# One input of the modulation products moved to PSUM in the first feed-forward, and the second parts of its up weights to GpSimd

## The chip, the cores and the metric

The kernel runs on one core of a Trainium2 chip. The metric is the device time of one execution in microseconds. A core has TensorE (PE, matmuls into PSUM; PEld is its loading of weights), VectorE (DVE), ScalarE (ACT), GpSimd (POOL), and SyncE (SP), which issues the DMAs here. SBUF is the working memory; PSUM is the memory that TensorE writes, used here as eight banks of 128 x 512 floats.

## The reference

Two layers over 512 latent tokens of width 1024; 256 context tokens go into the first layer's mixer only. Each layer scales and shifts its input by columns worked out from a vector c (the modulation), runs a mixer (gated DeltaNet and pooling in the first layer, convolutions in the second), normalizes, runs a feed-forward and normalizes again. What the change touches are the modulation and the first feed-forward:

```python
mod = silu_c @ ada_w[layer] + ada_b[layer]            # silu_c: 1024, ada_w: 1024 x 6144 for each layer
sh_m, sc_m, gt_m, sh_f, sc_f, gt_f = [m[:, None, :] for m in jnp.split(mod, 6, axis=-1)]
...
a, gate = jnp.split(u @ w_up, 2, axis=-1)             # w_up: 1024 x 5632
y = (jax.nn.silu(_dwconv2d_grid(a, conv_w)) * gate) @ w_down
```

The convolution is depthwise, 3 x 3, over the 512 tokens as a grid of 8 x 64.

## The kernel before

All arrays stand with channels on the 128 partitions and the 512 tokens along the row. A product of full precision is made of three matmuls in a reduced format: each weight and each activation is split into a first part (the value rounded to the format, names ending in hi or h) and a second part (what the rounding left, names ending in lo or l), and each 128 x 128 block of weights is multiplied as hi x h, hi x l, lo x h (`gemm`, line 219). A weight of the up projection is 128 x 1024 and comes in two pieces of 128 x 512. For each piece SyncE loads `w_raw` (line 159), ScalarE casts it to `w_hi` (line 167), and VectorE or GpSimd subtracts to get `w_lo` (line 173). Which of the two does it is dealt out by a counter: `self.share` is added for each piece, and when the counter reaches 1, VectorE gets the piece. Raw pieces, first parts and second parts have four buffers each.

Up projection of a feed-forward (`ffn`): 22 blocks m, each of two products, `pa` and `pg` (the first three products are made in two halves of 256 tokens, `half_ps`, so that they can start while the normalization before them still works on the second half). Of `pa`, ScalarE makes the middle tap into `f_acc` (line 578), VectorE adds the other eight taps (line 589), ScalarE takes the silu (line 591), VectorE multiplies by `pg` into `f_hid` (line 593), and ScalarE and GpSimd split that into `hh` (line 448) and `hl` (line 449; in the first eight blocks the tiles are called `ah` and `al`).

Modulation: the columns that the first mixer's input needs are made on TensorE at the start. The other 80 columns of 128 (`ada_rest`) are made on VectorE beside other work: a column's weights, 128 x 1024, come as two tiles `ada_w` (line 353), and for each a product with `crow` (the silu of c, the same row on each partition, in SBUF) is taken and summed along the row into one number per partition (line 354). That is one scalar_tensor_tensor with its sum written out, 160 in all; I call it a product here. 24 columns are made in the first mixer and its output projection. In the first feed-forward, blocks m = 2 to 21 make two columns each, so four products behind each `f_hid`, and the first six tiles of the down projection make the other 16. Their order on VectorE is pinned to the order of the program; the rest of the order on each engine is set by a scheduler when the program is built.

PSUM: the eight banks are two rings of four, "0" and "1". `bank` takes them in turn by a pattern of rings: products by "001" in a feed-forward, so two in ring 0 and one in ring 1, and the normalization's small results (`ln_e`, `ln_w`) from ring 1. A bank is free again when its last reader is done.

Down projection (`out_proj`): eight tiles, each over 22 weights; behind them the normalization, whose result goes into the second mixer's input. The shares are 0.1 in the first mixer, 0.35 and 0.5 in the two mixers' output projections, 0.4 in both feed-forwards with 0.5 at their end, 0.1 in the second mixer.

Of the kernel before, what the change touches and what calls it, by code (L numbers as in the profile page):

```python
# [15 lines left out]
T = 512  # L16
# [16 lines left out]
MUL, ADD, SUB = ALU.mult, ALU.add, ALU.subtract  # L33
# [13 lines left out]
SHARE = 0.4  # L47
SHARE_OUT = (0.35, 0.5)
SHARE_ODD = 0.1
SHARE_DOWN = 0.5  # L50
LAST = (4, 4)
LAST_FFN = 2
# [10 lines left out]
EVEN_RINGS = ("0", "1")  # L63
RINGS = ("001", "1")
RINGS_ODD = ("01", "1")
AX0 = 12
AX1 = 8
R2 = 1
# [47 lines left out]
class Kernel:  # L116
# [11 lines left out]
    def constants(self):  # L128
        nc, a = self.nc, self.a
        cp = self.cp = self.pool("const")  # L130
        self.cvec = cp.tile([P, KD, 2], F32, name="cvec")
        nc.sync.dma_start(out=self.cvec, in_=a["cvec"])
        prm = cp.tile([P, a["prm"].shape[1]], F32, name="prm")
        nc.sync.dma_start(out=prm, in_=a["prm"])
        for name, (o, shape) in PARAMS.items():
            n = math.prod(shape)
            v = prm[:, o:o + n]
            if len(shape) == 2:
                v = v.rearrange("p (a b) -> p a b", b=shape[1])
            if len(shape) == 3:  # L140
                v = v.rearrange("p (a b c) -> p a b c", b=shape[1], c=shape[2])
            setattr(self, name, v)
        self.ones = cp.tile([P, P], F32, name="ones")
        nc.vector.memset(self.ones, 1.0)
        self.onesn = cp.tile([P, 2], F32, name="onesn")
        nc.vector.memset(self.onesn, 1.0 / D)
        self.eps = cp.tile([P, 2], F32, name="eps")
        nc.vector.memset(self.eps[:, 0:1], LN_EPS)
        nc.vector.memset(self.eps[:, 1:2], RMS_EPS)

        self.mod = cp.tile([P, 2, 80], F32, name="mod")
        self.ada_next = 0
        self.crow = cp.tile([P, D], F32, name="crow")


# [187 lines left out]
    def ada_rest(self, n, pin=False):  # L343

        nc = self.nc
        if self.ada_next == 0:
            nc.sync.dma_start(out=self.crow, in_=self.a["crow"].broadcast_to([P, D]))
            nc.scalar.activation(out=self.crow, in_=self.crow, func=AF.Silu)
        for i in range(self.ada_next, self.ada_next + n):
            for k in range(2):  # L350
                w = self.ada_tile(k)
                cs = slice(T * k, T * k + T)
                nc.sync.dma_start(out=w, in_=self.a["ada1"][i][:, cs])
                r = nc.vector.scalar_tensor_tensor(out=w, in0=w, scalar=1.0, in1=self.crow[:, cs], op0=MUL, op1=MUL,  # L354
                                                   accum_out=self.mod[:, k, i:i + 1])
                if pin:
                    self.tc.keep_in_program_order(r)
        self.ada_next += n
# [139 lines left out]
    def out_proj(self, src, nk, xh, xl, gt, cols, uh, ul, ahead=0, between=None, ring=None, first=()):  # L498
# [35 lines left out]
        if nk != KD:  # L534
            self.share = SHARE_DOWN
        tick = lambda: norm and next(norm[0], 0)
# [23 lines left out]
    def ffn(self, layer, gt, cols):  # L560
        nc = self.nc
        with ExitStack() as ctx:
            fp = self.pool(f"ffn{layer}", ctx=ctx)
            ring = lambda nm: fp.tile([P, T], F32R, tag="h", bufs=2 * (KF - KD), name=nm)
            temp = lambda i, nm: fp.tile([P, T], F32, tag=("acc", "hid")[i], bufs=2, name=nm)
            self.ada_tile = lambda k: fp.tile([P, T], F32, tag="ada", bufs=ADA_FFN, name="ada_w")
            hh, hl = list(self.ah), list(self.al)
            up = self.a["ffn_up"]
            take = self.products([up[layer, KF * i + m] for m in range(KF) for i in range(2)], ring,
                                 FIRST[2 * layer])  # L570
            for m in range(KF):
                pa, pg = take(), take()
                if m >= KD:
                    hh.append(ring("hh"))
                    hl.append(ring("hl"))
                w = self.fconv[:, layer, m]
                acc = temp(0, "f_acc")
                nc.scalar.activation(out=acc, in_=pa, func=AF.Copy, scale=w[:, 4:5])  # L578
                av = acc.rearrange("p (r c) -> p r c", c=GW)
                sv = pa.rearrange("p (r c) -> p r c", c=GW)  # L580
                for dr in (-1, 0, 1):
                    for dc in (-1, 0, 1):
                        if dr == 0 and dc == 0:
                            continue
                        tap = 3 * (dr + 1) + dc + 1
                        r0, r1 = max(0, -dr), GR - max(0, dr)
                        q0, q1 = max(0, -dc), GW - max(0, dc)
                        o = av[:, r0:r1, q0:q1]
                        nc.vector.scalar_tensor_tensor(out=o, in0=sv[:, r0 + dr:r1 + dr, q0 + dc:q1 + dc],  # L589
                                                       scalar=w[:, tap:tap + 1], in1=o, op0=MUL, op1=ADD)  # L590
                nc.scalar.activation(out=acc, in_=acc, func=AF.Silu)  # L591
                hid = temp(1, "f_hid")
                nc.vector.tensor_tensor(out=hid, in0=acc, in1=pg, op=MUL)
                self.split(hid, hh[m], hl[m])
                next(self.late, 0)
                if layer == 0 and m >= ADA0:
                    self.ada_rest(int(ADA_RATE * (m + 1)) - int(ADA_RATE * m), True)
                if layer == 0 and m == KF - 1:
                    self.columns(1)

            def between(m):
                if layer == 0 and self.ada_next < 80:
                    self.ada_rest(min(ADN, 80 - self.ada_next), True)
                    if self.ada_next == 80:
                        self.columns(2)

            u = (None, None) if cols is None else (self.uh, self.ul)
            self.out_proj(self.a["ffn_down"][layer], KF, hh, hl, gt(), cols, *u, between=between)


    def even(self):
        nc, a = self.nc, self.a
        with ExitStack() as ctx:
# [11 lines left out]
            ps, pooled, self.decays = {}, [], {}  # L625
            left = [[AX0, AX1]]

# [545 lines left out]
    def odd(self):  # L1173
        nc, a = self.nc, self.a
        self.share = SHARE_ODD
        self.rings = RINGS_ODD
        with ExitStack() as ctx:
# [249 lines left out]
```

## Time and profile before

| what | value |
|---|---|
| three timed runs | 1387.52, 1382.17, 1387.93 us (median 1387.52) |
| profiled execution | 1384.9 us |
| its span | 1383.0 us, mean granted TensorE clock 0.967 |
| TensorE busy | 1286.8 us (93%) |
| VectorE busy | 990.9 us (72%) |
| GpSimd busy | 665.0 us (48%) |
| ScalarE busy | 579.8 us (42%) |
| chain that ended last | PE 62%, DVE 22% |
| in the chain by line | PE prod_ps 28%, PE out_ps 20%, DVE ada_w 6%, DVE f_acc 3% |

The span goes from the first to the last instruction of the profiled execution. The chain is followed back from the last instruction, at each step to what released it; the share of an engine in it is the time in which that engine, and nothing else, set the end. A row of a time line has its start and duration in us, the engine, the line of the kernel, the operation, output and input tiles with their shapes, and in brackets how long the engine was idle ahead of it and what ended that. The stages, in us of the span: first mixer to about 343, its output projection to 400, first feed-forward up to 682 and down to 808, second mixer to 961, its output projection to 1001, second feed-forward up to 1244 and down to the end.

### The profile page before, as it was taken

The page shows a single profiled execution, that of the slowest core. Times are in us where ns is not written, and L with a number is a line of the kernel's source. Part 1 is how long each engine was busy: PE and PEld are TensorE (multiplying, and loading weights), DVE is VectorE, ACT ScalarE, POOL GpSimd, SP SyncE. Part 2 cuts the span into 40 slices and gives each one's busy share as a digit, 9 for nine tenths or more (in the row PEclk, how much of TensorE's full clock was granted, in tenths as well). Part 3 has the DMA queues.
Part 4 walks back from the last instruction along what each step waited for, and adds up shares of the span by engine and source line. Part 5 has one row for each costly group of instructions (what it writes and reads, how often), then busy time and mean ns, then how long its engine had stood idle before and what let it go on. Part 6 is the DMA issues. An engine that isn't in the chain of part 4 may idle for free.

```text
span 1383.0 us, 19515 instructions
## 1 busy us (share of the span) xinstructions
PE 1286.8 (93%) x6690; PEld 1075.9 (78%) x6690; DVE 990.9 (72%) x1901; ACT 579.8 (42%) x1089; POOL 665.0 (48%) x580
## 2 busy tenths in 40 slices
PE   6898889989799998988899999899999999999997
PEld 2677878877698776777788888677988888888886
DVE  3388899998688999999955668775676666661125
ACT  3354423446456323323222367545473433332235
POOL 1345456665634444434345665973444344344453
PEclk9899999999899999999999999999999999999998
DMA  9521212430523455544466542232223333233334
GB/s 302 200 69 45 63 43 90 147 115 31 195 95 108 163 172 164 162 159 159 154 193 205 155 135 77 69 100 87 66 77 99 98 94 98 99 90 97 99 111 130
DMA packets 104947, 166.56 MB, mean 120 GB/s; under 512 B 20945, under 2 KB 29201, under 8 KB 104849
## 3 DMA queue, kind: packets, MB, share of 16 engines
q1 hardware_dynamic: 93888, 164.09, 37.5%
q10 hardware_dynamic: 10960, 1.25, 0.6%
q8 instruction: 52, 0.85, 0.2%
q14 instruction: 47, 0.38, 0.1%
HBM read 162.60 MB, written 2.69 MB: 120 GB/s over the span
## 4 chain that ended last, share of the span: by engine, by line
PE 62%; DVE 22%; issue 3%; POOL 3%; ACT 3%; DMA 2%; SPq 0%; ACTq 0%; POOLq 0%; DVEq 0%
PE prod_ps L219 28%; PE out_ps L219 20%; DVE ada_w L354 6%; DVE f_acc L589 3%; PE half_ps L219 3%; DVE w_lo L173 2%; PE ln_e L409 1%; PE qkv_ps L219 1%; PE it_ps L973 1%; PE gate_ps L219 1%; POOL w_lo L173 1%; PE dd_ps L848 1%; DVE z L470 1%; DVE x_t L919 1%; PE iv_ps L981 1%
## 5 line engine op out<-in xcount | busy, mean ns | idle before, releaser
L173 POOL TENSOR_TENSOR w_lo<-w_raw,w_hi 128x512 fp32r<-128x512 f32 (+1 forms) x263 | 358.2, 1368 | 407.9 <-ACT w_hi L167 386.8
L167 ACT CAST w_hi<-w_raw 128x512 fp32r<-128x512 f32 (+1 forms) x408 | 245.1, 607 | 431.0 <-PE prod_ps L219 147.9
L219 PE MATMUL prod_ps<-uh,w_lo 128*128 128x512 f32 x792 | 314.2, 397 | 26.8 <-DVE w_lo L173 20.5
L219 PE MATMUL prod_ps<-uh,w_hi 128*128 128x512 f32 x792 | 312.2, 394 | 0.0
L219 PE MATMUL prod_ps<-ul,w_hi 128*128 128x512 f32 x792 | 311.8, 394 | 0.0
L589 DVE SCALAR_TENSOR_TENSOR f_acc<-prod_ps,prm,f_acc 128x441 f32<-128x441 f32 (+2 forms) x320 | 222.0, 694 | 42.7 <-ACT f_acc L578 34.3
L173 DVE TENSOR_TENSOR w_lo<-w_raw,w_hi 128x512 fp32r<-128x512 f32 (+1 forms) x145 | 118.7, 819 | 126.6 <-ACT w_hi L167 123.3
L219 PEld LDWEIGHTS prod_ps<-uh,w_lo 128*128 128x128 f32 x792 | 151.2, 191 | 64.0 <-DVE w_lo L173 23.7
L354 DVE SCALAR_TENSOR_TENSOR ada_w<-ada_w,crow 128x512 f32<-128x512 f32 x160 | 174.6, 1139 | 4.0 <-DMA ada_w<-in_ada 3.8
L219 PEld LDWEIGHTS prod_ps<-uh,w_hi 128*128 128x128 f32 x792 | 151.3, 191 | 31.7 <-ACT w_hi L167 0.7
L219 PEld LDWEIGHTS prod_ps<-ul,w_hi 128*128 128x128 f32 x792 | 150.9, 191 | 32.0
L219 PE MATMUL out_ps<-ah,w_lo 128*128 128x256 f32 (+1 forms) x352 | 120.3, 342 | 10.0 <-DVE w_lo L173 10.0
L219 PE MATMUL out_ps<-ah,w_hi 128*128 128x256 f32 (+1 forms) x352 | 121.2, 345 | 4.7 <-ACT w_hi L167 3.1
L219 PE MATMUL out_ps<-al,w_hi 128*128 128x256 f32 (+1 forms) x352 | 121.3, 344 | 0.0
L219 PE MATMUL out_ps<-hh,w_lo 128*128 128x512 f32 (+1 forms) x280 | 99.4, 355 | 2.4 <-POOL w_lo L173 1.9
L219 PE MATMUL out_ps<-hh,w_hi 128*128 128x512 f32 (+1 forms) x280 | 98.7, 353 | 0.1
L219 PE MATMUL out_ps<-hl,w_hi 128*128 128x512 f32 (+1 forms) x280 | 98.5, 352 | 0.0
L219 PEld LDWEIGHTS out_ps<-ah,w_lo 128*128 128x128 f32 x352 | 69.0, 196 | 17.6 <-DVE w_lo L173 10.7
L219 PEld LDWEIGHTS out_ps<-ah,w_hi 128*128 128x128 f32 x352 | 68.9, 196 | 12.8 <-ACT w_hi L167 3.5
L449 POOL TENSOR_TENSOR hl<-f_hid,hh 128x512 fp32r<-128x512 f32 x28 | 40.9, 1461 | 75.3 <-ACT hh L448 75.3
L219 PEld LDWEIGHTS out_ps<-al,w_hi 128*128 128x128 f32 x352 | 69.3, 197 | 7.8 <-DVE al L449 0.6
L591 ACT ACTIVATE f_acc<-f_acc 128x512 f32<-128x512 f32 x44 | 27.8, 632 | 107.8 <-DVE f_acc L589 107.8
(359 smaller groups left out, 2316.6 us busy)
## 6 DMA issues: line engine op xcount, KB each, us to landing
ada_w<-in_ada SPq DMA_DIRECT2D x192, 256.0 KB, 3.0
w_raw<-in_ffn_up SPq DMA_DIRECT2D x176, 256.0 KB, 2.7
w_raw<-in_ffn_down SPq DMA_DIRECT2D x100, 256.0 KB, 2.7
w_raw<-in_even_in SPq DMA_DIRECT2D x40, 256.0 KB, 2.8
w_raw<-in_odd_in SPq DMA_DIRECT2D x40, 256.0 KB, 2.7
w_raw<-in_even_out SPq DMA_DIRECT2D x16, 256.0 KB, 2.9
w_raw<-in_odd_out SPq DMA_DIRECT2D x16, 256.0 KB, 2.7
w_raw<-in_ffn_down SPq DMA_DIRECT2D x20, 128.0 KB, 2.2
```

The lines of the kernel that those rows point to most:

```text
L167: r = nc.scalar.copy(out=hi[:, :n], in_=raw)
L173: r = eng.tensor_tensor(out=lo[:, :n], in0=raw, in1=hi[:, :n].bitcast(F32), op=SUB)
L219: r = nc.tensor.matmul(out=o, lhsT=w, rhs=x[k][:, c0:c1], start=clear and k == i == 0, stop=k == n - 1 and i == 2, skip_group_check=pin)
L354: r = nc.vector.scalar_tensor_tensor(out=w, in0=w, scalar=1.0, in1=self.crow[:, cs], op0=MUL, op1=MUL, accum_out=self.mod[:, k, i:i + 1])
L409: nc.tensor.matmul(out=pe[:, 2 * (n * e + i):2 * (n * e + i) + 2], lhsT=t[:, i * P:(i + 1) * P], rhs=ones, start=e == 0 and i == 0 and not ...
L449: (eng or nc.gpsimd).tensor_tensor(out=l, in0=x, in1=h.bitcast(F32), op=SUB)
L470: nc.vector.tensor_tensor(out=z, in0=z, in1=x, op=op)
L589: nc.vector.scalar_tensor_tensor(out=o, in0=sv[:, r0 + dr:r1 + dr, q0 + dc:q1 + dc], scalar=w[:, tap:tap + 1], in1=o, op0=MUL, op1=ADD)
L591: nc.scalar.activation(out=acc, in_=acc, func=AF.Silu)
L848: nc.tensor.matmul(out=o, lhsT=self.tri[:, 2 + d], rhs=r, start=d == 0, stop=d == 1)
L919: nc.vector.tensor_tensor(out=t, in0=a2[w, :, r, r + 1:16][:, :, None, :].broadcast_to([96, 2, m, m]), in1=x[w, :, r + 1:16, r + 1:16].rea ...
L973: nc.tensor.matmul(out=pt[:, h], lhsT=m[:, h], rhs=r1[:, h], start=True, stop=True)
```

## The change

In the first feed-forward alone, three things. Both halves of `crow` are copied by ScalarE into PSUM, into one bank of each ring, and the products there read them from PSUM in place of SBUF; the banks are held until the last product in the down projection. The share in the up stage becomes 0, so that GpSimd makes all `w_lo` of its up weights that are not made earlier; the counter stands still meanwhile. The pattern of rings for products in this feed-forward becomes "01", alternating, so that three banks of each ring are used in turn. Before and after, all lines of the file behind the change have other numbers (line 354 is 358, 173 is 176, 589 is 601, 593 is 605, 449 is 453).

```diff
+SHARE_ADA = 0
...
+RINGS_ADA = ("01", "1")
...
+        self.crow_ps = None
...
-                r = nc.vector.scalar_tensor_tensor(out=w, in0=w, scalar=1.0, in1=self.crow[:, cs], op0=MUL, op1=MUL,
+                c = self.crow_ps[k] if self.crow_ps else self.crow[:, cs]
+                r = nc.vector.scalar_tensor_tensor(out=w, in0=w, scalar=1.0, in1=c, op0=MUL, op1=MUL,
                                                    accum_out=self.mod[:, k, i:i + 1])
...
             up = self.a["ffn_up"]
+            if layer == 0:
+                self.rings = RINGS_ADA
+                self.share = SHARE_ADA
+                self.crow_ps = [self.bank(r, "crow_ps") for r in "01"]
+                for k, o in enumerate(self.crow_ps):
+                    nc.scalar.copy(out=o, in_=self.crow[:, T * k:T * k + T])
...
             self.out_proj(self.a["ffn_down"][layer], KF, hh, hl, gt(), cols, *u, between=between)
+            self.rings = RINGS
+            self.crow_ps = None
```

In the whole program VectorE has 145 of the 408 `w_lo` before and 109 after.

VectorE, one block in the middle of the first feed-forward's up stage, before; `ada_w` are the tiles of the products, `mod` takes their sums:

```order
L593 TENSOR_TENSOR f_hid<-f_acc,prod_ps 128x512
L354 SCALAR_TENSOR_TENSOR ada_w,mod<-ada_w,crow 128x512 x4
L173 TENSOR_TENSOR w_lo<-w_raw,w_hi 128x512
L589 SCALAR_TENSOR_TENSOR f_acc<-prod_ps,prm,f_acc 128x7x63
L589 SCALAR_TENSOR_TENSOR f_acc<-prod_ps,prm,f_acc 128x448
L589 SCALAR_TENSOR_TENSOR f_acc<-prod_ps,prm,f_acc 128x7x63
L589 SCALAR_TENSOR_TENSOR f_acc<-prod_ps,prm,f_acc 128x8x63 x2
L589 SCALAR_TENSOR_TENSOR f_acc<-prod_ps,prm,f_acc 128x7x63
L173 TENSOR_TENSOR w_lo<-w_raw,w_hi 128x512
L589 SCALAR_TENSOR_TENSOR f_acc<-prod_ps,prm,f_acc 128x448
```

The same place after:

```order
L605 TENSOR_TENSOR f_hid<-f_acc,prod_ps 128x512
L358 SCALAR_TENSOR_TENSOR ada_w,mod<-ada_w,crow_ps 128x512 x4
L601 SCALAR_TENSOR_TENSOR f_acc<-prod_ps,prm,f_acc 128x7x63
L601 SCALAR_TENSOR_TENSOR f_acc<-prod_ps,prm,f_acc 128x448
L601 SCALAR_TENSOR_TENSOR f_acc<-prod_ps,prm,f_acc 128x7x63
L601 SCALAR_TENSOR_TENSOR f_acc<-prod_ps,prm,f_acc 128x8x63 x2
L601 SCALAR_TENSOR_TENSOR f_acc<-prod_ps,prm,f_acc 128x7x63
L601 SCALAR_TENSOR_TENSOR f_acc<-prod_ps,prm,f_acc 128x448
```

The two `w_lo` are gone from among the products and taps; the products' second input is `crow_ps`, and the rest stands as it stood.

GpSimd, the same block, from one `hl` to the next, with the semaphores that each instruction waits for (Activation is ScalarE, DMAHW a load), before:

```order
L449 TENSOR_TENSOR hl<-f_hid,hh 128x512 [waits Activation_49]
L173 TENSOR_TENSOR w_lo<-w_raw,w_hi 128x512 [waits DMAHW2_49,PE_49,Activation_49]
L173 TENSOR_TENSOR w_lo<-w_raw,w_hi 128x512 [waits DMAHW3_49,PE_49,Activation_49]
L173 TENSOR_TENSOR w_lo<-w_raw,w_hi 128x512 [waits DMAHW1_49,PE_49,Activation_49]
L449 TENSOR_TENSOR hl<-f_hid,hh 128x512 [waits Activation_49]
```

After:

```order
L453 TENSOR_TENSOR hl<-f_hid,hh 128x512 [waits Activation_49]
L176 TENSOR_TENSOR w_lo<-w_raw,w_hi 128x512 [waits DMAHW2_49,PE_49,Activation_49]
L176 TENSOR_TENSOR w_lo<-w_raw,w_hi 128x512 [waits DMAHW3_49,PE_49,Activation_49]
L176 TENSOR_TENSOR w_lo<-w_raw,w_hi 128x512 [waits DMAHW4_49,PE_49,Activation_49]
L176 TENSOR_TENSOR w_lo<-w_raw,w_hi 128x512 [waits DMAHW5_49,PE_49,Activation_49]
L453 TENSOR_TENSOR hl<-f_hid,hh 128x512 [waits Activation_49]
```

Four `w_lo` stand between two `hl` where two or three stood. On ScalarE the order of a block is now the same for each: middle tap, casts of pieces 4m+6 and 4m+7, silu, cast of 4m+8, cast of `hid`, cast of 4m+9. On SyncE the four loads for the next block's products are followed by the raw pieces from 4m+13 on.

## The prediction

> **What bounds the kernel now.** I took the span first, then the chain of work that ended last, to see in which stage a unit other than TensorE sets the end. Its rows from the first feed-forward's up stage, and the one long row of the second feed-forward's:
>
> ```profile
> span 1383.0 us, 19515 instructions
> ...
> 423.02 32.23 PE prod_ps L219 x142
> ...
> 544.42 4.65 DVE ada_w L354 x8
> 549.07 1.66 DVE w_lo L173
> ...
> 1021.03 223.07 PE prod_ps L219 x984
> 1244.10 107.17 PE out_ps L219 x528
> ```
>
> The profiled execution took 1384.9 us, its span and 1.9 us around it; it lies 2.6 us under the median of the three timed runs, 1387.52. The second feed-forward's 984 matmuls of the up stage run without a break: 0.2267 us each, 10.88 us for the 48 of one block (a pair of weights). Up to 1351 us the chain there stays on TensorE. In the first feed-forward it goes over to VectorE again and again, in the modulation products (ada_w) and the second part (w_lo) behind them. The windows of both up stages, columns PE, PEld, DVE, ACT, POOL busy, granted clock, DMA share:
>
> ```profile
> 423.00:682.00 259.00, 233.75 (x987) 190.13 (x985) 239.68 (x375) 89.04 (x151) 109.26 (x71) 0.96 0.49 157
> 1021.00:1244.00 223.00, 223.00 (x986) 184.68 (x985) 151.37 (x226) 92.30 (x153) 91.94 (x71) 1.00 0.31 98
> ```
>
> The same matmuls take 259.0 us in the first and 223.1 in the second: 35.9 us that TensorE doesn't need. VectorE is busy for 239.7 us of the 259, so it is the bound there: 259.0 / 984 x 48 = 12.63 us a block. What TensorE waits for there, and what it does behind one such wait:
>
> ```profile
> PE prod_ps L219 <- DVE w_lo L173: 20.5, 5, 5.5
> PE out_ps L219 <- DVE w_lo L173: 4.5, 1, 4.5
> ...
> 550.78 0.80 PE L219 MATMUL prod_ps<-uh,w_lo 128*128 128x512 f32 x1 [5.47 <-DVE w_lo L173]
> 551.38 0.63 PE L219 MATMUL prod_ps<-uh,w_hi 128*128 128x512 f32 x1
> 551.80 0.63 PE L219 MATMUL prod_ps<-ul,w_hi 128*128 128x512 f32 x1
> 554.67 0.39 PE L219 MATMUL prod_ps<-uh,w_hi 128*128 128x512 f32 x1
> ```
>
> Six waits, 25.0 us. Behind the wait the matmuls start 0.42 us apart, for some 3 us, and then run in 0.39 us again: that slow restart, six times, is the other 11 us (the granted clock over the stage is 0.96 against 1.00). All 25.0 us go to a w_lo made by VectorE. Why it is late, in VectorE's and GpSimd's time lines of one block:
>
> ```profile
> 543.81 0.69 DVE L593 TENSOR_TENSOR f_hid<-f_acc,prod_ps 128x512 f32<-128x512 f32 x1 [0.76 <-ACT f_acc L591]
> 544.42 0.68 DVE L354 SCALAR_TENSOR_TENSOR ada_w<-ada_w,crow 128x512 f32<-128x512 f32 x1
> 545.03 0.69 DVE L354 SCALAR_TENSOR_TENSOR ada_w<-ada_w,crow 128x512 f32<-128x512 f32 x1
> 545.64 1.75 DVE L354 SCALAR_TENSOR_TENSOR ada_w<-ada_w,crow 128x512 f32<-128x512 f32 x1
> 547.32 1.74 DVE L354 SCALAR_TENSOR_TENSOR ada_w<-ada_w,crow 128x512 f32<-128x512 f32 x1
> 548.99 1.74 DVE L173 TENSOR_TENSOR w_lo<-w_raw,w_hi 128x512 fp32r<-128x512 f32 x1
> ...
> 545.24 1.60 POOL L449 TENSOR_TENSOR hl<-f_hid,hh 128x512 fp32r<-128x512 f32 x1 [7.24 <-ACT hh L448]
> 546.81 3.37 POOL L173 TENSOR_TENSOR w_lo<-w_raw,w_hi 128x512 fp32r<-128x512 f32 x2
> ```
>
> Two products run in 0.68 us while GpSimd rests; from 545.24, when GpSimd works, products and w_lo take 1.75, and GpSimd's own 1.6 to 1.7 each. Both inputs of each of these stand in SBUF. Against that, the second feed-forward, where VectorE's taps and its f_hid read one input from PSUM:
>
> ```profile
> 1101.05 3.66 DVE L589 SCALAR_TENSOR_TENSOR f_acc<-prod_ps,prm,f_acc 128x504 f32<-128x504 f32 x5
> 1105.47 0.69 DVE L593 TENSOR_TENSOR f_hid<-f_acc,prod_ps 128x512 f32<-128x512 f32 x1 [0.76 <-ACT f_acc L591]
> 1109.21 5.09 DVE L589 SCALAR_TENSOR_TENSOR f_acc<-prod_ps,prm,f_acc 128x441 f32<-128x441 f32 x7
> ...
> 1103.21 1.30 POOL L173 TENSOR_TENSOR w_lo<-w_raw,w_hi 128x512 fp32r<-128x512 f32 x1 [4.19 <-ACT w_hi L167]
> 1106.02 1.29 POOL L173 TENSOR_TENSOR w_lo<-w_raw,w_hi 128x512 fp32r<-128x512 f32 x1 [1.52 <-ACT w_hi L167]
> 1111.37 1.29 POOL L173 TENSOR_TENSOR w_lo<-w_raw,w_hi 128x512 fp32r<-128x512 f32 x1 [2.80 <-ACT w_hi L167]
> ```
>
> GpSimd works inside the taps, and neither is slowed: taps at 0.73 us, GpSimd at 1.30.
>
> **The change, part by part.** The rows for the prices, from the groups of lines of the first up stage (count, busy, mean ns), the page, and VectorE's time line at the end of the down stage:
>
> ```profile
> L354 DVE SCALAR_TENSOR_TENSOR ada_w<-ada_w,crow 128x512 f32<-128x512 f32 x76 | 88.0, 1212 | 0.0
> L173 DVE TENSOR_TENSOR w_lo<-w_raw,w_hi 128x512 fp32r<-128x512 f32 x32 | 29.8, 931 | 0.8 <-ACT w_hi L167 0.7
> ...
> L578 ACT ACTIVATE f_acc<-prod_ps,prm 128x512 f32<-128x512 f32 x20 | 13.6, 682 | 0.0
> ...
> L167 ACT CAST w_hi<-w_raw 128x512 fp32r<-128x512 f32 (+1 forms) x408 | 245.1, 607 | 431.0 <-PE prod_ps L219 147.9
> w_raw<-in_ffn_up SPq DMA_DIRECT2D x176, 256.0 KB, 2.7
> ...
> 775.73 0.75 DVE L516 SCALAR_TENSOR_TENSOR z<-out_ps,mod,z 128x512 f32<-128x512 f32 x1 [2.84 <-PE out_ps L219]
> 777.01 1.77 DVE L354 SCALAR_TENSOR_TENSOR ada_w<-ada_w,crow 128x512 f32<-128x512 f32 x1
> ```
>
> *Products with crow in PSUM.* No row shows one with its sum and this operand. Bounds: 0.61 us from start to start (the 0.68 rows undisturbed) and 1.75 (still held up). Nearest are f_hid (0.69, second input in PSUM) and z (0.75, the same instruction from PSUM). I take 0.70. VectorE's block is then 8 taps of 0.73 (5.8), the pause 0.76 for ScalarE's silu, f_hid 0.61 (to the next start), four products 2.8: 10.0 us, under TensorE's 10.88. The w_lo are gone from it (29.8 us of the stage); the products' 88.0 us become about 53.
>
> *All w_lo of the up weights on GpSimd.* Each costs 1.30 us there against 0.68 on VectorE; five GpSimd instructions a block make 6.5 of 10.88 us. The Trainium skill's "GPSIMD Engine Reference" (section Engine selection) speaks against this: elementwise work with two inputs belongs on VectorE, GpSimd being about 2 times slower; the rows agree (1.9 times). By it alone the 36 moved ones cost 36 x 0.62 = 22 us, if nothing covered them.
>
> Cover: let A be the end of a block's first product. A piece is half a weight, 12 matmuls, 2.72 us, and four pieces are held; ScalarE may cast piece 4m+5 at A, 4m+6 at A+2.7, 4m+7 at A+5.4, 4m+8 at A+8.2, each when TensorE leaves the buffer. In its order, first cast, initial tap (0.7), two casts, silu, cast, cast of hid, none of these comes more than 0.7 us late: the taps run from A+1.3 to A+7.1, silu to A+7.8, f_hid to A+8.4, products to A+11.2, and the next taps need A+12.2. GpSimd has the w_lo of 4m+8 at A+10.1, hl at A+11.4, and the w_lo of 4m+9, cast at A+11.5, at A+12.8: 1.9 us behind the buffer, where TensorE needs it 8.2 behind. So 6 us of cover. SyncE: behind the four loads for products, which wait for VectorE until A+11.2, stands the load of piece 4m+13, which waits anyway for the w_lo of 4m+9 (A+12.8); it lands 2.7 us later, with the cast due at A+21.8. TensorE becomes the bound: 35.9 us go.
>
> *Two banks fewer.* The two copies of crow hold one bank of each ring until the last product. A bank of a first product is free at A+7.1, and with three left in each ring the third next block asks for it, at A+27: nothing.
>
> *The two copies on ScalarE*, during the normalization ahead of the stage: each between 0.61 and 0.68 us, the cast's and the initial tap's prices; one stands where ScalarE waits, the other is counted, 0.6. The ring that loses a bank there puts half products behind the second ln_w: I add 0.5 (from -2 to +2; the stretch has 1.2 us of idle TensorE now):
>
> ```profile
> 409.31 0.70 PE L419 MATMUL ln_w<-ln_d,ones 128*128 128x256 f32 x2 [1.22 <-DVE ln_d L416]
> ...
> PE prod_ps L219 <- POOL w_lo L173: 6.0, 6, 2.0
> ```
>
> *The last products* (777.01) stand on the chain that ends the down stage: 1.77 becomes 0.7, -1.1. *Later shares:* the counter that deals out w_lo comes out of the stage at another value, so that in the second mixer and behind other w_lo fall to VectorE; the last row above is what TensorE waits there (6.0 us): from -4 to +4, taken as 0. For the stage's ramp, where VectorE finishes two f_hid in a row, I keep 1.6 (0 to 5).
>
> Sum: 1384.9 - 35.9 - 1.1 + 0.6 + 0.5 + 1.6 = 1350.6, say 1351; own range 1343 to 1360.
>
> **The rivals.** B: the PSUM operand helps only in part, and two products of a block are still held, as now, 1.07 each: VectorE's block is 12.1 us against 12.63, over 20.5 blocks (984 / 48) -11, so 1374. Against it: the taps beside GpSimd. For it: no row shows the product itself. C: GpSimd's w_lo come late in place of VectorE's, since they stand behind hl, which waits for VectorE's f_hid: if the 6 us of cover are gone in each block, the six waits stay under another name, 1385. Against it: GpSimd is busy for 109 of 259 us. D, slower: the operand frees nothing, and since GpSimd now works without a pause at A+8.4 to A+12.8, three or four of the four products are held: 10.0 + 3 x 1.07 = 13.2 or 14.3 us a block, 1397 to 1419, say 1405. It decides from 12.63 on, that is from the third held product.
>
> The Trainium skill's "SBUF — State Buffer" (section Who interferes with whom) says that a VectorE instruction with at most one SBUF input, outside its two-port modes, does not contend with GpSimd. By that rule B and D can't come; the taps' rows agree, the accumulating form is not shown.
>
> **How the numbers follow.** Forecast 0.78, B 0.09, C 0.08, D 0.05. A measurement of this kernel tells about 0.5% from no change, 7 us. Faster: forecast and most of B, 0.86; same: C and the rest of B, 0.09; slower: D, 0.05. Range: 1343 to 1374, which takes in B and leaves out C and D.
>
> **What would show it.** Right: TensorE's waits in the first up stage near 0, its 984 matmuls in 223 to 228 us at a clock near 1.00; products at one duration, 0.68 to 0.77, no second mode at 1.75; GpSimd's hl at 1.30 instead of 1.60; VectorE waiting for the initial tap. Wrong: products above 1 us (B, D); TensorE waiting for w_lo of GpSimd (C); a stretch from 400 to 423 us longer by over 3, or the second mixer by over 4.

## The result, and the profile after

The changed kernel takes 1340.52 us (median of four runs, 1339.57 to 1342.02) against 1384.85 us for the kernel before (four runs): a ratio of 0.9681, 95% interval 0.9651 to 0.9711. That is 44 us less where 34 were forecast, and 2.5 us below the low end of the range, 1343. The profiled execution took 1340.33 us. From the page, the span and two rows of the chain:

```profile
span 1338.5 us, 19585 instructions
...
426.13 223.05 PE prod_ps L222 x984
649.18 107.17 PE out_ps L222 x528
```

The up stage of the first feed-forward is now one unbroken row, like that of the second one before (223.07), and the first 528 matmuls of the down stage follow without a break. The next two tables cut both programs at the first matmul of each stage: the three products made in halves, up, down with the normalization behind it, the halves of the second mixer, its other products, its output projection. A row has its window and its length, then PE, PEld, DVE, ACT, POOL busy (with the number of instructions), the granted clock, the DMA share and GB/s. Before:

```profile
400.70:422.80 22.10, 20.15 (x158) 19.24 (x159) 15.66 (x33) 16.72 (x37) 10.37 (x11) 1.00 0.40 129
422.80:676.80 254.00, 233.26 (x985) 190.09 (x985) 234.65 (x368) 87.55 (x149) 104.87 (x69) 0.96 0.49 157
676.80:815.90 139.10, 132.02 (x690) 112.72 (x689) 90.55 (x158) 49.44 (x93) 74.25 (x59) 0.96 0.55 174
815.90:836.20 20.30, 19.67 (x158) 19.00 (x158) 11.31 (x29) 15.49 (x33) 12.99 (x12) 1.00 0.34 105
836.20:942.30 106.10, 100.09 (x442) 80.50 (x441) 81.93 (x119) 54.65 (x90) 78.87 (x64) 0.98 0.27 85
942.30:1000.10 57.80, 55.14 (x318) 48.65 (x318) 38.38 (x74) 26.44 (x49) 22.85 (x17) 0.91 0.25 78
```

After:

```profile
401.00:425.90 24.90, 22.88 (x158) 21.54 (x158) 15.70 (x34) 18.64 (x41) 14.63 (x14) 0.86 0.35 109
425.90:648.90 223.00, 223.00 (x986) 184.80 (x986) 178.74 (x346) 90.12 (x148) 129.87 (x101) 1.00 0.58 186
648.90:775.90 127.00, 126.83 (x690) 109.37 (x689) 63.86 (x145) 47.93 (x88) 60.14 (x52) 1.00 0.58 175
775.90:798.00 22.10, 20.09 (x159) 19.30 (x158) 12.44 (x29) 15.74 (x32) 14.81 (x16) 1.00 0.39 120
798.00:898.90 100.90, 97.66 (x442) 79.63 (x440) 82.39 (x120) 55.03 (x91) 79.78 (x64) 1.00 0.29 90
898.90:955.90 57.00, 55.04 (x318) 48.97 (x318) 36.29 (x73) 26.50 (x49) 22.99 (x17) 0.91 0.24 78
```

Row by row the change is +2.8, -31.0, -12.1, +1.8, -5.2 and -0.8 us: -44.5, the whole difference of the spans (1383.0 to 1338.5). So only two thirds came from the up stage; 12 us came from the down stage and 4 from the second mixer with its output projection, whose lines the change doesn't touch.

VectorE and GpSimd in one block of the up stage after the change:

```profile
542.67 0.69 DVE L605 TENSOR_TENSOR f_hid<-f_acc,prod_ps 128x512 f32<-128x512 f32 x1 [0.81 <-ACT f_acc L603]
543.27 0.68 DVE L358 SCALAR_TENSOR_TENSOR ada_w<-ada_w,crow_ps 128x512 f32<-128x512 f32 x1
...
546.92 5.81 DVE L601 SCALAR_TENSOR_TENSOR f_acc<-prod_ps,prm,f_acc 128x441 f32<-128x441 f32 x8 [1.14 <-ACT f_acc L590]
553.54 0.69 DVE L605 TENSOR_TENSOR f_hid<-f_acc,prod_ps 128x512 f32<-128x512 f32 x1 [0.82 <-ACT f_acc L603]
```

```profile
543.66 1.29 POOL L176 TENSOR_TENSOR w_lo<-w_raw,w_hi 128x512 fp32r<-128x512 f32 x1 [1.43 <-ACT w_hi L170]
544.91 1.30 POOL L453 TENSOR_TENSOR hl<-f_hid,hh 128x512 fp32r<-128x512 f32 x1
546.38 1.29 POOL L176 TENSOR_TENSOR w_lo<-w_raw,w_hi 128x512 fp32r<-128x512 f32 x1 [0.17 <-ACT w_hi L170]
```

From one f_hid to the next are 10.87 us, TensorE's pace; VectorE now waits 1.14 us for the middle tap, so its own work is 9.73 us a block where I had 10.0, and GpSimd waits for casts. The products run beside GpSimd's work in 0.68 us and GpSimd's instructions in 1.30. All 112 products of the feed-forward, from its tile's answer:

```profile
L358 DVE SCALAR_TENSOR_TENSOR ada_w<-ada_w,crow_ps x112: 677/683/689, 445.1 to 742.0; 128x512 f32<-128x512 f32 x112
```

The shortest takes 677 ns, the median 683, the longest 689: one duration, where the same 112 took 678 to 1786 ns before.

TensorE's waits from 682 to 1001 us before, and over the same work after (649 to 956):

```profile
PE prod_ps L219 <- POOL w_lo L173: 6.0, 6, 2.0
PE out_ps L219 <- DVE w_lo L173: 5.0, 3, 4.5
PE ln_e L409 <- DVE ln_s L393: 2.4, 1, 2.4
PE out_ps L219 <- POOL w_lo L173: 1.9, 1, 1.9
```

```profile
PE prod_ps L222 <- POOL w_lo L176: 2.6, 2, 1.9
PE ln_e L413 <- DVE ln_s L397: 2.0, 1, 2.0
PE ln_w L423 <- DVE ln_d L420: 1.9, 2, 1.5
```

The 4.5 us at the start of the down stage (VectorE's w_lo behind the up stage's last products) are gone, but so are the 1.9 us for a w_lo of GpSimd at the end of that stage, and 3.4 of the 6.0 us in the mixer. What a wait costs beside its own length is seen at two of them before: windows of the wait, of the stretch behind it, and of what follows:

```profile
545.31:550.60 5.29, 0.00 (x0) 0.00 (x0) 5.29 (x7) 1.98 (x4) 4.87 (x3) 1.00 0.57 159
550.60:554.01 3.41, 3.23 (x8) 2.56 (x9) 3.27 (x6) 0.00 (x0) 0.00 (x0) 0.50 0.84 246
554.01:558.00 3.99, 3.99 (x19) 3.31 (x18) 3.16 (x6) 1.26 (x2) 1.43 (x1) 1.00 0.30 106
680.31:687.13 6.82, 5.14 (x12) 4.08 (x13) 6.64 (x9) 0.62 (x1) 1.28 (x2) 0.50 0.48 153
```

The granted clock is 0.50 for 3.41 us behind the first (8 matmuls in place of 15, so 1.7 us lost) and for 6.82 us from the middle of the second on (that wait ends at 681.99, so 5.1 us of the stretch lie behind it, and 2.6 us are lost). By the trace's record of the clock there are five such stretches in the up stage before, 20.5 us long in all, of which 2.5 us lie inside the waits, where half a clock costs nothing: 9.0 us lost. The windows have the whole: TensorE is busy for 233.26 us before and for 223.00 after, 10.3 us more for the same matmuls, and idle for 20.7 us before and not at all after, together the 31.0 that went. The 1.3 us that the slow stretches leave over are in part the start behind each wait, slower at the full clock, too: behind the wait of 2.63 us that ends at 576.96 the next matmul starts 0.34 us later, not 0.23.

### The profile page after: what moved, and what is told of

It is laid out like the page before. It is cut to its first block, busy times and chain, and to the rows that moved or that the text cites. A ratio compares the mean times of both kernels' runs of the same rounds, so it can differ in the third digit from the quotient of the medians.

```text
span 1338.5 us, 19585 instructions
## 1 busy us (share of the span) xinstructions
PE 1271.3 (95%) x6690; PEld 1069.2 (80%) x6690; DVE 907.3 (68%) x1865; ACT 583.9 (44%) x1091; POOL 680.5 (51%) x616
## 4 chain that ended last, share of the span: by engine, by line
PE 73%; DVE 11%; POOL 4%; issue 3%; ACT 2%; DMA 2%; SPq 0%; ACTq 0%; POOLq 0%; DVEq 0%
PE prod_ps L222 37%; PE out_ps L222 22%; PE half_ps L222 3%; DVE ada_w L358 2%; POOL w_lo L176 1%; PE qkv_ps L222 1%; POOL conf_far L1221 1%; PE ln_e L413 1%; PE it_ps L987 1%; PE gate_ps L222 1%; PE dd_ps L862 1%; DVE x_t L933 1%; DMA ada_w<-in_ada 1%; POOL cb_t L886 1%; PE ln_w L423 1%
## 5 line engine op out<-in xcount | busy, mean ns | idle before, releaser
L176 POOL TENSOR_TENSOR w_lo<-w_raw,w_hi 128x512 fp32r<-128x512 f32 (+1 forms) x299 | 385.0, 1292 | 449.8 <-ACT w_hi L170 441.5
L222 PE MATMUL prod_ps<-uh,w_lo 128*128 128x512 f32 x792 | 308.9, 390 | 2.6 <-POOL w_lo L176 2.6
L222 PE MATMUL prod_ps<-uh,w_hi 128*128 128x512 f32 x792 | 308.7, 390 | 0.6 <-ACT w_hi L170 0.6
L222 PE MATMUL prod_ps<-ul,w_hi 128*128 128x512 f32 x792 | 308.4, 389 | 0.0
L176 DVE TENSOR_TENSOR w_lo<-w_raw,w_hi 128x512 fp32r<-128x512 f32 (+1 forms) x109 | 87.0, 799 | 137.7 <-ACT w_hi L170 135.1
L358 DVE SCALAR_TENSOR_TENSOR ada_w<-ada_w,crow_ps 128x512 f32<-128x512 f32 x112 | 70.8, 683 | 8.7 <-DMA ada_w<-in_ada 8.7
L222 PEld LDWEIGHTS out_ps<-hl,w_hi 128*128 128x128 f32 x280 | 52.7, 188 | 7.7
L222 PEld LDWEIGHTS out_ps<-hh,w_lo 128*128 128x128 f32 x280 | 52.6, 188 | 7.7
```

The source lines that it names most:

```text
L176: r = eng.tensor_tensor(out=lo[:, :n], in0=raw, in1=hi[:, :n].bitcast(F32), op=SUB)
L222: r = nc.tensor.matmul(out=o, lhsT=w, rhs=x[k][:, c0:c1], start=clear and k == i == 0, stop=k == n - 1 and i == 2, skip_group_check=pin)
```

## The experiments

My theory (M in the texts below) was that the PSUM operand frees VectorE's products from GpSimd, and that this ends the up stage's waits. The rivals were that the share does it, and, since 10 us came that I hadn't forecast, two for these: the down stage's own products, or the deal of later w_lo (theory P). That deal is made by a counter; with share 0 it stands still in the up stage and leaves it at 0.6 where it was 0.8 before, and from there on other pieces go to VectorE.

**Crow in PSUM, share as before** (edit of the changed kernel):

```diff
-SHARE_ADA = 0
+SHARE_ADA = 0.4
```

> Crow in PSUM and the rings of the changed kernel, but the up weights' second parts dealt out as before (share 0.4), so the counter, too, runs on as before. Theory M (VectorE's block): 10.0 us without w_lo, plus 1.6 w_lo a block of 0.61 to 1.7 us each, so 11.0 to 12.7 us against TensorE's 10.88: the up stage's 984 matmuls take 225 to 240 us, the kernel 1343 to 1358. Rival 1, the operand does everything and the share nothing: up stage 223 us, 1338 to 1343. Rival 2, the share does the main part: up stage above 245 us, 1365 or more. If the second mixer's gain hangs on the counter, its products take 102 us again, otherwise 97.

It took 1344.95 us, ratio 0.9728 (0.9714 to 0.9743). The up stage's window, and VectorE's groups in it:

```profile
425.40:648.40 223.00, 223.00 (x987) 184.67 (x986) 195.01 (x379) 90.72 (x149) 90.96 (x71) 1.00 0.58 185
```

```profile
L358 DVE SCALAR_TENSOR_TENSOR ada_w<-ada_w,crow_ps 128x512 f32<-128x512 f32 x76 | 47.6, 682 | 0.0
L176 DVE TENSOR_TENSOR w_lo<-w_raw,w_hi 128x512 fp32r<-128x512 f32 x32 | 22.0, 689 | 10.1 <-ACT w_hi L170 10.0
```

VectorE makes its 32 w_lo at 689 ns (931 before) and TensorE waits for none. The operand alone, with its rings and held banks, makes the stage TensorE's: rival 1 for the stage, though the kernel's time lies above rival 1's range. From the first start to the last, the mixer's 408 products took 102.3 us again (102.4 before, 97.2 in the changed kernel), so that gain does hang on the counter.

**Share 0 alone** (edit of the kernel before):

```diff
+            if layer == 0:
+                self.share = 0
             take = self.products([up[layer, KF * i + m] for m in range(KF) for i in range(2)], ring,
```

> Share 0 in the first up stage alone; crow stays in SBUF, rings as before. Theory M: three or four products of each block meet GpSimd's row of w_lo and take 1.75 us, 13.2 to 14.3 us a block on VectorE: the up stage takes 270 to 293 us against 254 before, the kernel 1400 to 1425, slower. Rival: VectorE is rid of 30 us of w_lo and only two products are held, 12.1 us a block, about 245 us and 1374, faster.

It took 1388.92 us, ratio 1.0038 (1.0020 to 1.0057): a little slower. Its up stage, and VectorE from one f_hid on:

```profile
423.80:694.50 270.70, 239.92 (x985) 184.37 (x984) 248.35 (x333) 83.80 (x146) 156.08 (x100) 0.98 0.47 148
```

```profile
540.53 0.69 DVE L595 TENSOR_TENSOR f_hid<-f_acc,prod_ps 128x512 f32<-128x512 f32 x1 [0.81 <-ACT f_acc L593]
541.14 1.72 DVE L354 SCALAR_TENSOR_TENSOR ada_w<-ada_w,crow 128x512 f32<-128x512 f32 x1
...
546.18 1.77 DVE L354 SCALAR_TENSOR_TENSOR ada_w<-ada_w,crow 128x512 f32<-128x512 f32 x1
...
554.48 0.69 DVE L595 TENSOR_TENSOR f_hid<-f_acc,prod_ps 128x512 f32<-128x512 f32 x1 [0.81 <-ACT f_acc L593]
```

All four products are held, 13.95 us a block: theory M's stage came, 270.7 us against 254.0. The profiled execution was the slowest of the seven, 1394.67 us. The kernel's time stayed under my 1400: the counter's gain came here too (the mixer's products took 99.2 us from first to last start), the down stage took 133.7 us against 139.1, and the stretch ahead of the up stage 20.9 us against 22.1. TensorE waited 29.6 us in the up stage (16.1 for ScalarE's casts, 13.5 for w_lo of GpSimd), most of it for 1.2 us or less at a time, and the clock stood at 0.98, where 20.5 us of longer waits had left it at 0.96 before.

**Half of the products** (first product of each pair from SBUF):

```diff
-                c = self.crow_ps[k] if self.crow_ps else self.crow[:, cs]
+                c = self.crow_ps[k] if self.crow_ps and k else self.crow[:, cs]
```

> The changed kernel, but the first product of each pair reads crow from SBUF, the second from PSUM. Theory M: two of four products are held, about 1.07 us each, 10.0 + 2.1 = 12.1 us a block on VectorE, up stage 243 to 250 us, the kernel 1360 to 1372. Rival: GpSimd's work between is short and only one or none is held, up stage under 235 us and under 1353.

It took 1339.96 us, ratio 0.9681 (0.9661 to 0.9701), the same as the changed kernel, with the up stage at 223.0 us; I had expected 243 to 250, so this forecast failed. Four products in a row:

```profile
537.06 1.74 DVE L358 SCALAR_TENSOR_TENSOR ada_w<-ada_w,crow 128x512 f32<-128x512 f32 x1
...
538.74 0.68 DVE L358 SCALAR_TENSOR_TENSOR ada_w<-ada_w,crow_ps 128x512 f32<-128x512 f32 x1
...
539.35 1.17 DVE L358 SCALAR_TENSOR_TENSOR ada_w<-ada_w,crow 128x512 f32<-128x512 f32 x1
...
540.44 0.68 DVE L358 SCALAR_TENSOR_TENSOR ada_w<-ada_w,crow_ps 128x512 f32<-128x512 f32 x1
```

In one row, beside the same work of GpSimd, SBUF operands give 1.74 and 1.17 and the PSUM operand 0.68: the operand is the cause. My sum a block (12.1) was too high; it is 11.2 from one f_hid to the next. That is still 0.3 over TensorE's 10.88, a lag that grows to some 5 us over the stage, and TensorE waits for none of it. With no w_lo in VectorE's queue a late VectorE holds only its own products' banks; that this is the reason was not tried by itself.

**The rings and the held banks alone** (a single column reads the banks, which keeps them held):

```diff
-SHARE_ADA = 0
+SHARE_ADA = 0.4
...
-                c = self.crow_ps[k] if self.crow_ps else self.crow[:, cs]
+                c = self.crow_ps[k] if self.crow_ps and i == 75 else self.crow[:, cs]
```

> The changed kernel's rings and its two held banks, with share 0.4, but the products read crow from SBUF (a single column of the down stage reads the banks, so that they stay held). Theory: two banks fewer cost nothing, the up stage takes 250 to 256 us as before, the kernel 1381 to 1388. Rival: three banks in each ring are too few beside late taps, and the time rises by over 5 us.

1385.15 us, ratio 1.0013 (1.0000 to 1.0026). TensorE's waits in the up stage are nearly the old ones (20.5 us before), and two banks fewer cost next to nothing there (255.0 us against 254.0):

```profile
PE prod_ps L222 <- DVE w_lo L176: 21.3, 5, 5.5
```

**The down stage's products from SBUF again:**

```diff
+            self.crow_ps = None
             def between(m):
```

> The changed kernel, but the 36 products of the down stage read crow from SBUF as before; those of the up stage read it from PSUM. Theory D1 (the down stage's lost 11 us were the backlog that the up stage left on VectorE): the down stage stays at 127 us from its first matmul to the last of the last tile, the kernel within 1338 to 1343. Rival D2 (they were the down stage's own products, held to 1.77 us): 3 to 11 us come back, 1343 to 1351.

1341.43 us, ratio 0.9699 (0.9680 to 0.9718): D1. The edit turns 32 products back, not 36 as I wrote. Down and normalization take 128.3 us against 127.0, with one wait of 0.8 us for a w_lo of VectorE. So the 4.5 us wait was what the up stage had left on VectorE. The last products, for which I had counted 1.1 us, gave 1.3 by this window and 0.9 by the medians, which is within the spread of the runs.

**The counter put back** behind the changed up stage:

```diff
+            if layer == 0:
+                self.nl = 0.799999999999999
             def between(m):
```

> The changed kernel, but behind the up stage the counter that deals out w_lo is set to the value that it has there before the change (0.8), so that every later w_lo is on the same engine as before. Theory P (the later gains hang on who gets which w_lo): the wait of 1.9 us in the normalization and those of the second mixer come back, with the clock's slow stretches behind them; the stretch from the start of the mixer's products takes 102 us against 97, the kernel 1345 to 1348. Rival: the later gains come of the earlier stage's end, and nothing changes, 1339 to 1342.

1348.91 us, ratio 0.9758 (0.9739 to 0.9777): 8.4 us of the result are gone. TensorE's waits from 649 to 963 us, and the mixer's products:

```profile
PE prod_ps L222 <- POOL w_lo L176: 6.1, 6, 1.9
PE ln_e L413 <- DVE ln_s L397: 2.4, 1, 2.4
PE out_ps L222 <- POOL w_lo L176: 1.9, 1, 1.9
```

```profile
799.40:905.70 106.30, 100.21 (x443) 80.55 (x441) 82.02 (x119) 54.53 (x90) 78.86 (x64) 0.98 0.28 85
```

The waits of before are back within 0.1 us, and the mixer takes its 106 us. Theory P holds. Not all came back in this execution: behind the wait of 1.9 us the clock didn't fall, and down with its normalization took 129.4 us, 2.4 more than with the counter at 0.6. The time is 0.9 us above the range that I had given.

**The counter alone**, in the kernel before:

```diff
+            if layer == 0:
+                self.nl = 0.5999999999999991
             def between(m):
```

> The kernel before, with one number set: behind the first up stage the counter that deals out w_lo is put to 0.6, the value that it has there after the change, so that only later w_lo change engines. Theory P (8 us of the result came of the deal of later w_lo): the 408 products of the second mixer take 97 us against 102, the down stage loses the wait of 1.9 us and the slow stretch behind it; in all 6 to 9 us less, 1375 to 1378. Rival: the later stages gain only where the first up stage leaves VectorE free, and the time stays at 1382 to 1386.

1370.27 us, ratio 0.9905 (0.9884 to 0.9926): 13 us for one number that changes hardly any work (VectorE makes 144 of the w_lo in place of 145). The mixer's products take 96.6 us from first to last start, and from 676 to 955 us TensorE's waits for w_lo are

```profile
PE out_ps L219 <- DVE w_lo L173: 4.6, 3, 3.2
PE prod_ps L219 <- POOL w_lo L173: 2.3, 2, 1.6
...
PE out_ps L219 <- POOL w_lo L173: 0.4, 1, 0.4
```

The time is 4.7 us below the range that I had given. Here the backlog of 4.6 us at the start of the down stage is split into shorter waits, and the clock doesn't fall behind them (1.00 over that stage, 0.96 before). Another 3.0 us went from the second output projection (54.8 us against 57.8, clock 0.95 against 0.91); why, I didn't follow up.

**Crow in PSUM, share as before, counter at 0.6**, run twice:

```diff
-SHARE_ADA = 0
+SHARE_ADA = 0.4
...
+            if layer == 0:
+                self.nl = 0.5999999999999991
             def between(m):
```

> Crow in PSUM with the share of before (0.4) in the up stage, and behind it the counter at the value that the changed kernel has there (0.6). If the share adds nothing to the operand, and the deal of later w_lo is worth 4 to 8 us by itself: 1337 to 1341, at or below the changed kernel's 1340.5, since the share of 0 slows the stretch ahead of the up stage (24.8 to 25.5 us against 22.9). Rival (the share has a part of its own): 1343 to 1346.

> Crow in PSUM, share 0.4 in the up stage, counter at 0.6 behind it, once more. If the share of 0 only costs at the stage's ramp (24.8 to 25.5 us against 22.9 to 23.1): 1335 to 1338, 3 to 5 us under the changed kernel. Rival: the two are the same within 2 us.

> The changed kernel itself once more, beside the next one on one chip, for the interval: 1339 to 1343.

1336.10 us, ratio 0.9661 (0.9644 to 0.9678), and 1337.36 us, ratio 0.9671 (0.9653 to 0.9690), beside the changed kernel's 1341.50, ratio 0.9700 (0.9684 to 0.9715). In eight runs it took 1334.5 to 1339.4 us, in nine the changed kernel took 1339.6 to 1342.4. It is the fastest kernel here, the first time 0.9 us below the range that I had given: the share of 0 adds nothing to the operand, and all that it did for the time it did through the counter. Its stretch ahead of the up stage, to be held against the changed kernel's row from 401.00 to 425.90:

```profile
400.90:424.10 23.20, 21.72 (x158) 20.46 (x158) 16.55 (x35) 18.24 (x40) 11.30 (x11) 0.93 0.39 125
```

With share 0 GpSimd is busy there for 14.6 us in place of 11.3, the clock is 0.86 in place of 0.93, and the stretch is 1.7 us longer. That the clock falls here at all goes with the rings and held banks, not with the share: all eleven traces that have them show a slow stretch of 3.41 or 6.83 us that begins between 405 and 410 us, and the three without (the kernel before, share 0 alone, the counter alone) show none. The rings alone took 24.6 us here at a clock of 0.86 (22.1 and 1.00 before), share 0 alone 20.9 us at 1.00. With share 0 the slow stretch was 6.83 us in six of seven traces, with 0.4 it was 3.41 us in three of four; whether the share makes it longer isn't settled.

**More work for GpSimd** (two or four more instructions a block):

```diff
                 self.split(hid, hh[m], hl[m])
+                if layer == 0:
+                    for _ in range(2):
+                        x = fp.tile([P, T], F32, tag="extra", bufs=1, name="extra")
+                        nc.gpsimd.tensor_tensor(out=x, in0=hid, in1=hl[m].bitcast(F32), op=ADD)
```

> The changed kernel with two more GpSimd instructions (128 x 512, two inputs in SBUF) behind each hl of the first up stage; their output isn't used. GpSimd then has 7 x 1.30 = 9.1 us in a block of 10.88, and the last w_lo stands 2.6 us later, 4.5 us behind its buffer where TensorE needs it 8.2 behind. Theory (the cover is 6 us): no wait, up stage 223 us, 1339 to 1344. Rival (GpSimd's row has no such cover): TensorE waits for w_lo of GpSimd, the up stage takes over 226 us, 1345 or more.

> The same with four more: 9 x 1.30 = 11.7 us a block, 0.8 above TensorE's 10.88. Theory: GpSimd is the bound of the stage; over 20 blocks 17 us, less what the cover still takes up, so the up stage takes 232 to 242 us, with TensorE waiting for w_lo of GpSimd about once a block for 1 us or less; as in the run with share 0 alone, waits that short need not slow the clock: 1349 to 1359. Rival: the clock is halved behind them, over 250 us and 1367 or more; or the lag never reaches TensorE, 1339 to 1344.

Two more: 1342.52 us, ratio 0.9711 (0.9696 to 0.9725), up stage 223.1 us, no wait. Four more: 1357.97 us, ratio 0.9826 (0.9803 to 0.9848); window of the up stage and TensorE's waits in it:

```profile
423.70:666.20 242.50, 229.12 (x986) 183.15 (x985) 179.82 (x345) 91.21 (x148) 231.31 (x182) 1.00 0.53 168
```

```profile
PE prod_ps L222 <- POOL w_lo L176: 13.4, 20, 2.0
```

GpSimd is busy for 231 of 242 us and TensorE waits for it once a block, mostly 0.6 us at a time; the clock stays at 1.00. So there is a cover, and two instructions (2.6 us) fit in it. With four GpSimd itself is past TensorE's pace (11.7 us a block by my sum against 10.88), so this run doesn't measure the cover: that it is 6 us isn't shown.

## Why the prediction was wrong, point by point

- **What bounds the stage, and that the operand frees it: right.** TensorE's waits went to none, the 984 matmuls to 223 us, products to 0.68, hl to 1.30. The tests of the operand (half of the products, share 0 alone) show it as the cause, and the Trainium skill's "SBUF — State Buffer" (section Who interferes with whom), which I had weighed against rivals B and D, agrees: 112 products with their sum written out, none above 689 ns. Rival D's block was priced well (13.2 to 14.3, measured 13.95 with share 0 alone) for a kernel in which the operand frees nothing.
- **That C wouldn't come: right.** TensorE waits for no w_lo of GpSimd in the stage, and the cover holds with two more instructions a block; its size of 6 us isn't shown.
- **"35.9 us go" in the up stage: right in size, cut at the wrong place.** My window ended at 682 us and so held the first 5.2 us of the down stage with its wait of 4.5. Up itself gave 31.0. The slow stretch behind that wait runs to 687.13, 5.1 us past my window at half clock: 2.6 us that I left out. In the rows I quoted for the slow restart I also set two different things side by side: 0.42 us is the time from one start to the next, 0.39 the duration of one matmul; at the full clock the starts are 0.23 us apart.
- **The step that failed: "later shares ... from -4 to +4, taken as 0".** I put this term of the sum at nothing, with 4 us as the most it could bring, and it measured -8.4: the counter put back took the changed kernel from 1340.5 to 1348.9 us by the medians (by the ratios to the kernel before, 0.9681 and 0.9758, it is 10.7). In the profile of the changed kernel that is 1.9 us of wait and 1.7 of slow clock at the end of the down stage, and 4.2 us from there to the end of the second output projection, 7.8 in one execution. Without it the kernel takes 1348.9 us, where I had 1351; that lies inside the range.
- **Why the bound was too narrow.** I took as the most that could go the one row of waits that I had quoted, 6.0 us, and less. The row of 1.9 us (out_ps for GpSimd's w_lo) was a wait of the same kind, and behind both the clock is at 0.50 for 3.41 us, at 810.0 and 919.2: 6.0 + 1.9 + 1.7 + 1.7 = 11.3. I had told of the slow restart for the up stage and didn't price it here. With -11 as the lower end the range would have begun near 1336 and held the result.
- **The ramp and the rings: right in sum, by luck.** Ahead of the up stage, where TensorE was idle for 1.95 us before and not for 1.2 as I read, I had 1.1 and it was 2.8; the rings and held banks alone, for which I allowed from -2 to +2 there, made that stretch 2.5 us longer, with a slow clock. The 1.6 inside the stage didn't come.

## What to carry to other kernels

Where VectorE and GpSimd work beside each other, try one input of VectorE's two-input instructions in PSUM if a bank is free: here it was worth 39 us without the share, and handing the work to GpSimd nothing by itself. A wait of TensorE of about 2 us cost here up to nearly twice its length, where the clock behind it was halved, so bound what a shifted deal of work may gain or lose by all waits of its kind and the slow stretches behind them. And when a change moves a counter, test the counter alone: one number was worth 8 to 13 us.

## What the runs showed of the hardware

- The granted clock falls to 0.50 for 3.41 or 6.83 us behind idle time of TensorE. Counted over the traces of all these runs, between 425 and 930 us, with a fall that begins no later than 3.5 us behind the idle time's end: of 19 idle times of 2.57 to 5.52 us, 18 were followed by one, of 15 from 1.86 to 2.16 us nine, of 19 from 1.44 to 1.64 us none. The Trainium skill's "TensorE: Matmul & The Clock Gate" (section Part 1: The HAM clock gate) gives windows of 3413 ns that run freely, and that length agrees. Its table lets the clock fall after at least one idle window of some 3.4 us; here 1.87 us was enough, and the measurement decides. Two things besides such idle times brought a fall. With share 0 alone, idle times of 1.20 and 0.62 us in quick succession were followed by one twice (557.3 and 584.6). And in 13 of the 14 traces the clock falls with no idle time ahead of it, during or within 1 us behind the 32 matmuls of two columns each (`ln_e`) that follow the second mixer's products: in the changed kernel they run from 895.47 to 898.96, TensorE counts as busy, and the clock is at 0.50 for 3.41 us from 899.10 on.
- Short waits can leave the clock alone and still cost more than their length: with four more GpSimd instructions a block TensorE waited 20 times, 13.4 us, at a clock of 1.00, and was busy for 229.12 us in place of 223.00, so 0.3 us more for each wait. The first start behind such a wait is 0.34 us ahead of the next, where it is 0.23 in the run of matmuls. By the length of the waits that is about as dear as before, when five waits of 20.5 us cost 10.3 us more.
- VectorE's and GpSimd's instructions with both inputs in SBUF exclude each other, and the row of half of the products shows it to the instruction. GpSimd beside it:

```profile
536.96 1.30 POOL L176 TENSOR_TENSOR w_lo<-w_raw,w_hi 128x512 fp32r<-128x512 f32 x1 [3.29 <-ACT w_hi L170]
538.21 1.75 POOL L453 TENSOR_TENSOR hl<-f_hid,hh 128x512 fp32r<-128x512 f32 x1
```

The product issued at 537.06 ends at 538.80, 0.54 behind the end of the w_lo (538.26); hl, issued at 538.21, ends at 539.96, 1.16 behind that product; the next product from SBUF, issued at 539.35, ends at 540.52, 0.56 behind hl. Each first lets the other finish, and then takes its own time, less a little. The product from PSUM between them (538.74 to 539.42) runs inside hl and waits for nothing.
